# Four early pairs of feature tiles in a decoder-layer kernel, their low parts left by accumulating DMAs

## The chip, the cores and the metric

The kernel runs on one core of a Trainium2 chip. The metric is the device time of one execution in microseconds (us), as the median of several runs. In the profile, PE is the matrix engine (TensorE), PEld its weight loads, DVE the vector engine, ACT the scalar engine, POOL the GpSimd engine and SP the engine that issues the kernel's DMAs.

## What is computed

One decoder layer on x of 512 tokens by 1024 features, in float32. Cut to what matters here:

```python
def reference(x, ...):
    mix = hybrid_mixer(x, w_in, ...)                # attention (8 heads) and a gated MLP (8 groups), then w_out
    x = layer_norm(ALPHA * x + mix, ln1_g, ln1_b)   # the first layer norm
    ffn = (silu(x @ w_gate) * (x @ w_up)) @ w_down  # hidden width 2816: 22 feature tiles of 128
    return layer_norm(ALPHA * x + ffn, ln2_g, ln2_b)
```

## The kernel before, in words

**Precision.** Each float32 operand is split in two float32r parts, high = round(a) and low = a - high, and a product is three matmuls: high by high, high by low, low by high. `split` (lines 234 to 241) issues the two operations: an ACT copy for the high part (line 238), and a subtraction on DVE or POOL for the low part (line 239; POOL with `far=True`). `mm3` (lines 243 to 249) is the three matmuls of the projections (lines 245 to 247).

**Stages.** In order of time: the projections v, q, k, z, u mixed with attention and the gated MLP; the output projection in two halves, `out_half(4, ...)` for the gated MLP and `out_half(0, ...)` for attention; the first layer norm, token tile by token tile (`layer_norm`, lines 679 to 713, called from `pa_done`, line 746), with transposes of the normalised rows (line 760) and splits of them; gate and up projections; down projection; the second layer norm.

**The attention half.** `pa_done` adds the projection, scaled by the token's RMS factor `ra[t]`, to xk (line 750). `ra[t]` comes from four calls of `rsqrt_col` (line 672): a small DVE operation (line 274) and a power operation on POOL (line 275) for each token tile. The letter of `LN1 = "APAD"` for token tile t says who normalises it: A and P use ACT (line 700) and then DVE for the gain (line 702), with the bias added on DVE (A) or POOL (P) at line 711; D uses DVE alone (lines 696 and 707).

**Gate and up projection.** The 22 feature tiles go in 11 pairs. A pair's weights are four blocks of 128x1024 (`Raw`, 512 KB each: a11, a21, a22, a12), and a pair takes seven products of 24 matmuls each (`product`, matmuls at line 838) in the manner of Strassen and Winograd: P1, P2, p5, p6, p3, p7, q4. Each has an operand made from the normalised tokens: P1 (`b11`) and P2 (`b21`) need only token tiles 0 and 1; `b22`, `n1`, `n2`, `t3` and `t4` need tiles 2 and 3 and the sums of `combine` (lines 728 to 741). The product P1 goes to a PSUM bank X, is copied by ACT to a tile `a` with the tag "cs" (line 860), and P2 is added on top in X; ACT's silu (line 865) and a DVE product (line 866) follow. P1 and P2 use the raw blocks a11 and a12; the other five use block sums (`grow`, line 933) or raw blocks. A split block takes one of three buffers "wh" and one of three "wl".

**Early pairs.** The first two pairs have P1 and P2 made ahead of the loop over pairs (lines 908 to 913), so that PE has them to do while the layer norm of token tiles 2 and 3 and `combine` go on. Their split blocks have buffers of their own, left by attention and the gated MLP ("pth" and "ptl" for the high parts, "znh" and "znl" for the low ones), and all four low parts are made on POOL (`EPOOL`). The raws of pair 0 and 1 come in through two "wr" buffers and two slots of "zg"; pair 0's a11 and a12 stay in their buffers for the loop. The loop then makes P1 and P2 for pairs 2 to 10 only.

**Order.** No instruction order is written by hand. Each operation is entered with an engine, a cost in us and a rank, and `Order.plan` (lines 107 to 177) simulates the five queues as a list scheduler: an engine that is free takes the ready operation with the lowest rank. The order in which the operations are issued, and with it each engine's in-order queue, is fixed by these planned costs. `MM = 0.643` is the planned cost of one `mm3`, a DMA has 1.9 us of latency after its issue, and tiles of one tag wait in the order of their creation for a buffer to come free.

Of the kernel before, what the change touches and what calls it, by code (L numbers as in the profile page):

```python
# [6 lines left out]
F32 = mybir.dt.float32  # L7
F32R = mybir.dt.float32r
AF = mybir.ActivationFunctionType
# [20 lines left out]

SAME, CROSS, DMA_LAT, MM, MM256 = 0.15, 0.19, 1.9, 0.643, 0.36
SEQ = ('q1', 'a1', 'q0', 'z', 'q2', 'a0', 'u', 'q3', 's', 'a2', 'a3')
RANK = {"w": 5.0, "rope": 10.0, "att": 4.0, "gelu": -8.0, "z": -2.0, "s": -13.5, "fill": 15.0, "sq": -6.0, "ln": -10.5, "ffn": 8.0, "evac": 3.0}


UNITS = (2, 0, 3, 1)
NORM = "AADA"
LN1, LN2, LNT = "APAD", "ADAD", 0.3  # L40
WHI = ('o0', 'o2', 'q1')
WPOOL = ('e0', 'e1', 'e3', 'o1', 'o2', 'o4', 'z')
ROPE, ZSUB, ZMUL, ZG, ZB = "P", "P", "P", "P", "P"
# [18 lines left out]
class Order:  # L62
# [11 lines left out]
        b.name = f"{b.tag}_{self.uid}"  # L74
        return b

    def op(self, eng, cost, fn, r=(), w=(), base=None, table=None, lock=False):
        o = Op()
        o.eng, o.cost, o.fn, o.table, o.lock = eng, cost, fn, table, lock
        o.lat = DMA_LAT if eng == "SP" else 0.0  # L80
        o.prio = (self.base if base is None else base, len(self.ops))
        o.deps, o.succ, o.bufs = set(), [], []
        for keys, writes in ((r, False), (w, True)):
            for key in keys:
                b, sub = key if isinstance(key, tuple) else (key, None)
                if not b.users:
                    self.bufs.append(b)
                if not b.users or b.users[-1] is not o:
                    b.users.append(o)
                    o.bufs.append(b)  # L90
                for s, x in b.writers.items():
                    if x is not o and (s is None or sub is None or s == sub):
                        o.deps.add(x)
                if writes:
                    for s, xs in b.readers.items():
                        if s is None or sub is None or s == sub:
                            o.deps.update(x for x in xs if x is not o)
                    if sub is None:
                        b.writers, b.readers = {None: o}, {}
                    else:  # L100
                        b.writers[sub], b.readers[sub] = o, []
                else:
                    b.readers.setdefault(sub, []).append(o)
        self.ops.append(o)
        return o
# [80 lines left out]
def build(tc, cp, wp, ap, ps, xt, xtok, w_vqk, w_zu, w_out, w_gu, w_dn, wsp, cst, rows, cols, out):  # L186
# [8 lines left out]
    def dve(n, fn, r, w, per=1.042, **k):  # L195
        od.op("DVE", 0.066 + 0.001 * per * n, fn, r, w, **k)
# [10 lines left out]
    def const(shape, tag=None, dtype=F32):  # L207
        return od.buf(cp, shape, dtype, tag)
# [10 lines left out]
    def small(n):  # L219
        return work([P, n], "sm", 24)  # L220

    def bank(tag, bufs):
        return od.buf(ps, [P, S], F32, tag, bufs)
# [10 lines left out]
    def split(n, src, hi, lo, rs, ws_hi, ws_lo, far=False, lock=True, near=False, **k):  # L234
        if near:
            dve(n, lambda: V.tensor_scalar(hi(), src(), 1.0, None, op0=ALU.mult), rs, ws_hi, per=0.52, lock=True, **k)
        else:
# [2 lines left out]
                                                                 op=ALU.subtract), [*rs, *ws_hi], ws_lo,  # L240
               lock=lock, **k)

    def mm3(cost, o, lh, ll, rh, rl, start, stop, r, w, **k):
        def fn():
            PE.matmul(o(), lhsT=lh(), rhs=rh(), start=start, stop=False)  # L245
            PE.matmul(o(), lhsT=lh(), rhs=rl(), start=False, stop=False)  # L246
            PE.matmul(o(), lhsT=ll(), rhs=rh(), start=False, stop=stop)  # L247

        pe(cost, fn, r, w, **k)
# [27 lines left out]


    ident, tri = const([P, P]), const([P, 2 * P])
    cosT, sinT = od.buf(cp, [P, S], F32, "cs", 2), od.buf(cp, [P, S], F32, "cs", 2)  # L280
    colp, rowp = const([P, 12]), const([P, 3, S])
    mhalf, ones = const([P, 32]), const([P, 2])
    dve(32, lambda: V.memset(mhalf.t, -0.5), [], [mhalf])
# [6 lines left out]
        return b  # L290


    zero, idle = const([P, S], dtype=mybir.dt.bfloat16), bank("pv", 1)
    dve(256, lambda: V.memset(zero.t, 0.0), [], [zero], base=-9)

    def warm():
# [350 lines left out]
    out_half(4, "zg", sg_left, pg_done)  # L647


    sb, ra = bank("tp", 1), [small(1) for _ in range(NT)]  # L650
    at2 = work([P, 2, NT, S], "xh", 1, F32R)

    def at_split(f):
# [14 lines left out]

    pe(0.45, sums, [sqa, ones], [sb], base=RANK["s"])
    od.base = RANK["att"]  # L670
    for t in range(NT):
        rsqrt_col(ra[t], lambda t=t: sb.t[:, t:t + 1], [sb], 1, 1.0 / 512, RMS_EPS)
    od.base = RANK["fill"]

    LN = [row(0), row(1)]
# [70 lines left out]
    def pa_done(t, b):  # L746
        ts = slice(t * P, t * P + P)

        def add(i, key):
            dve(560, lambda: V.scalar_tensor_tensor(out=xk.t[:, t, HV[i]], in0=b[i].t, scalar=ra[t].t,  # L750
                                                    in1=xk.t[:, t, HV[i]], op0=ALU.mult, op1=ALU.add),
                [b[i], ra[t], key], [key])

        def done(i, key):
            tp = bank("tp", 1) if i == 0 else bank("pv", 1)

            def turn():
                for j in range(4):
                    js = slice((4 * i + j) * P, (4 * i + j + 1) * P)
                    PE.transpose(tp.t[:, j * P:j * P + P], xk.t[:, t, js], ident.t)  # L760

            pe(0.45, turn, [*key, ident], [tp])
            xr = XR[i, t] = prob() if t < 2 else tmp()
            act(512, lambda: A.activation(xr.t, tp.t, AF.Copy), [tp], [xr])
            if t < 2 or i == 1:
                opnd_split(("b11", "b21")[i] if t < 2 else "b22", t % 2,
                           lambda: tp.t.rearrange("p (k c) -> p k c", c=P), [tp], False)
            if t >= 2 and i == 1:
                combine(t - 2)

        od.base = RANK["ln"] + LNT * t
        layer_norm(t, add, done, LN1[t])
        od.base = RANK["fill"]
# [22 lines left out]
    class Raw:  # L796


        def __init__(self, p, j, slot):
            if slot in ("wr", "kl"):  # L800
                b = od.buf(wp, [P, WCH], F32, "wr", 2) if slot == "wr" else work([P, WCH], "kl", 2)
                self.t, self.key = (lambda c=slice(0, WCH): b.t[:, c]), b
            else:
                self.t, self.key = (lambda c=slice(0, WCH): zgr.t[:, slot, c]), (zgr, slot)
            dma(512, lambda: nc.sync.dma_start(self.t(), w_gu[4 * p + j]), [], [self.key], base=PREP)

    class Blk:


        def __init__(self, early=None):  # L810
            if early is None:
                h, l = od.buf(wp, [P, WCH], F32R, "wh", 3), od.buf(wp, [P, WCH], F32R, "wl", 3)
                self.lo, self.lk = (lambda c: l.t[:, c]), l
            else:
                h, l = work([P, WCH], ("pth", "ptl")[early // 2], 2, F32R), early_lo[early // 2]
                self.lo, self.lk = (lambda c: l.t[:, early % 2, c]), (l, early % 2)
            self.hi, self.hk = (lambda c: h.t[:, c]), h
# [6 lines left out]
            return self  # L824

    def whole(raw, early=None):
        return Blk(early).fill(raw.t, raw.key, far=early in EPOOL)

    def product(blk, name, bank, first):
        buf, s = OPND[name]  # L830
# [15 lines left out]
    class Pair:  # L846
# [4 lines left out]
            (self.h0, self.i0), (self.h1, self.i1) = hT[2 * p], hT[2 * p + 1]  # L851

        def begin(self):
            self.a = od.buf(cp, [P, S], F32, "cs", 2)
            self.X = pj()

        def p1(self, blk):
# [47 lines left out]
            self.gated(c, self.h1, self.i1, 0, -1.0)  # L905

    pairs = [Pair(p) for p in range(NP)]
    EARLY, EPOOL = 2, (0, 1, 2, 3)
    first = [[Raw(0, 0, "wr"), Raw(0, 3, "wr")], [Raw(1, 0, 0), Raw(1, 3, 1)]]
    for p in range(EARLY):  # L910
        blks = [whole(r, 2 * p + i) for i, r in enumerate(first[p])]
        pairs[p].p1(blks[0])
        pairs[p].p2(blks[1])
    RING = ("kl", "kl", "wr", "wr", 0, 1)
    held_back = None
    for p, pair in enumerate(pairs):
        if p == 0:
            a11, a12 = first[0]
            a21, a22 = Raw(0, 1, 0), Raw(0, 2, 1)
        else:  # L920
            a11, a21, a22, a12 = (Raw(p, j, RING[(4 * (p - 1) + j) % 6]) for j in range(4))
        if p >= EARLY:
            pair.p1(whole(a11))

        acc = [bank("tp", 1), bank("pv", 1)]
        s1 = Blk()

        def grow(blk, one, two):
            for side in range(2):
                def step(side=side, o=acc[side]):  # L930
                    x = (lambda: o.t) if two is None else (lambda: two.t(HALF[side]))
                    k = [o] if two is None else [two.key]
                    dve(512, lambda: V.tensor_tensor(out=o.t, in0=x(), in1=one.t(HALF[side]), op=ALU.add),
                        [one.key, *k], [o], lock=two is not None, base=PREP)
                    blk.fill(lambda: o.t, o, 512, 512 * side, lock=False)

                step()

        grow(s1, a21, a22)
        pool(1024, lambda a=a11, b=a21: PL.tensor_tensor(out=b.t(), in0=a.t(), in1=b.t(), op=ALU.add),  # L940
             [a11.key, a21.key], [a21.key], base=PREP)
        pair.p5(s1)
        if held_back:
            held_back[0].q4(held_back[1])
        s2 = Blk()
        grow(s2, a11, None)
        pair.p6(s2)
        if p >= EARLY:
            pair.p2(whole(a12))
        s4 = Blk()  # L950
        grow(s4, a12, None)
        pair.p3(s4)
        pair.p7(whole(a21))
        held_back = pair, whole(a22)
# [123 lines left out]
```

## Time and profile before

| | |
|---|---|
| median of 3 runs | 570.67 us (569.95 to 571.86) |
| the profiled execution's own time | 570.17 us |
| its span in the trace | 568.1 us |
| PE busy | 547.5 us, 96% of the span |
| DVE busy | 413.2 us, 73% |
| ACT busy | 280.9 us, 49% |
| POOL busy | 157.0 us, 28% |

The profile is of one execution. The span runs from its first to its last recorded instruction; times inside it are counted from the span's start. Busy shares are averages over stages with different limits, so the stage around the first layer norm is read from windows and timelines of its own.

### The profile page before, as it was taken

Reading aid. Unit: us, or ns where it says so; the run is one execution under the profiler, and the core shown is the slowest. Engines: PE = TensorE matmul, PEld = TensorE weight load, DVE = VectorE, ACT = ScalarE, POOL = GpSimd, SP = SyncE. Lnnn points to the kernel's source line nnn. Section 1 sums busy time; section 2 is a strip of 40 time slices with the busy share of each in tenths; the row PEclk is TensorE's granted clock in tenths of the full one; section 3 lists DMA queues with packets and bytes.
Section 4 is the critical chain, followed back from the end, with each engine's and each line's share of the span. In section 5 each row is a group of like instructions: output and inputs, shape, how many; then the busy total and the mean of one; then the engine's idle time right before and its main releaser. Section 6 shows DMA issues by size and latency. Waiting matters only on the chain.

```text
span 568.1 us, 8774 instructions
## 1 busy us (share of the span) xinstructions
PE 547.5 (96%) x3360; PEld 488.6 (86%) x3360; DVE 413.2 (73%) x707; ACT 280.9 (49%) x482; POOL 157.0 (28%) x119
## 2 busy tenths in 40 slices
PE   9999999999899968999999999999999999999994
PEld 5888888887688857999999999999999888888883
DVE  5537779879975699998788788888877723334385
ACT  6323796788864347544545544544455422323211
POOL 0026258613205730253333242343322200000011
PEclk9999999999999979899999999999999999999998
DMA  7745514155715201432332333333124332232311
GB/s 260 265 131 153 140 48 129 43 163 182 226 38 194 102 3 72 144 127 103 112 112 76 115 109 109 116 111 112 38 75 149 112 111 94 92 112 74 112 74 74
DMA packets 21225, 65.51 MB, mean 115 GB/s; under 512 B 2880, under 2 KB 3392, under 8 KB 21184
## 3 DMA queue, kind: packets, MB, share of 16 engines
q1 hardware_dynamic: 21184, 64.96, 34.6%
q8 instruction: 26, 0.43, 0.3%
q14 instruction: 15, 0.12, 0.1%
HBM read 58.66 MB, written 2.10 MB: 107 GB/s over the span
## 4 chain that ended last, share of the span: by engine, by line
PE 94%; DVE 2%; ACT 2%; issue 0%; POOL 0%; DVEq 0%
PE pj L838 22%; PE sc L838 17%; PE pj L245 12%; PE pj L247 12%; PE pj L246 12%; PE sc L245 2%; PE sc L247 2%; PE sc L246 2%; PE pv L481 2%; PE tp L464 1%; PE sc L426 1%; PE pv L247 1%; PE pv L245 1%; PE tp L247 1%; PE tp L245 1%; PE tp L246 1%
## 5 line engine op out<-in xcount | busy, mean ns | idle before, releaser
L239 DVE TENSOR_TENSOR wl<-wr,wh 128x1024 fp32r<-128x1024 f32 (+1 forms) x55 | 71.8, 1306 | 60.7 <-ACT wh L238 60.1
L238 ACT ACTIVATE wh<-wr 128x1024 fp32r<-128x1024 f32 (+1 forms) x58 | 57.8, 999 | 84.4 <-PE sc L247 54.0
L838 PE MATMUL pj<-qk,wh 128*128 128x256 f32 x352 | 65.6, 287 | 1.2 <-ACT wh L238 1.2
L838 PE MATMUL sc<-xh,wh 128*128 128x256 f32 x352 | 64.5, 284 | 0.0
L838 PEld LDWEIGHTS pj<-qk,wh 128*128 128x128 f32 x352 | 55.8, 195 | 1.4 <-ACT wh L238 1.4
L838 PEld LDWEIGHTS sc<-xh,wh 128*128 128x128 f32 x352 | 55.1, 193 | 0.0
L275 POOL TENSOR_TENSOR sm<-sm,only 128x1 f32<-128x1 f32 (+1 forms) x20 | 16.4, 825 | 137.8 <-DVE sm L274 137.7
L838 PE MATMUL pj<-V,wh 128*128 128x256 f32 x288 | 52.6, 283 | 0.0
L838 PE MATMUL pj<-qk,wl 128*128 128x256 f32 x176 | 50.7, 288 | 0.4 <-DVE wl L239 0.4
L838 PE MATMUL sc<-xh,wl 128*128 128x256 f32 x176 | 49.8, 283 | 0.0
L245 PE MATMUL pj<-wh,xh 128*128 128x512 f32 x114 | 46.3, 406 | 0.0
L838 PEld LDWEIGHTS pj<-V,wh 128*128 128x128 f32 x288 | 44.9, 192 | 0.0
L246 PE MATMUL pj<-wl,xh 128*128 128x512 f32 x114 | 44.6, 391 | 0.0
L838 PE MATMUL pj<-V,wl 128*128 128x256 f32 x144 | 40.8, 283 | 0.0
L247 PE MATMUL pj<-wh,xl 128*128 128x512 f32 x96 | 37.7, 393 | 0.0
L239 POOL TENSOR_TENSOR wl<-wr,wh 128x1024 fp32r<-128x1024 f32 x7 | 17.2, 2456 | 72.8 <-ACT wh L238 67.9
L838 PEld LDWEIGHTS pj<-qk,wl 128*128 128x128 f32 x176 | 34.3, 195 | 0.8 <-DVE wl L239 0.8
L838 PEld LDWEIGHTS sc<-xh,wl 128*128 128x128 f32 x176 | 33.9, 192 | 0.0
L238 ACT ACTIVATE wh<-tp 128x512 fp32r<-128x512 f32 x33 | 19.7, 596 | 27.9 <-PE sc L838 26.0
L838 PE MATMUL sc<-ug,wh 128*128 128x256 f32 x176 | 32.1, 283 | 0.0
L239 DVE TENSOR_TENSOR wl<-tp,wh 128x512 fp32r<-128x512 f32 x33 | 22.6, 684 | 8.6 <-ACT wh L238 8.6
L245 PE MATMUL pj<-wh,pr 128*128 128x512 f32 x72 | 28.0, 389 | 0.0
(331 smaller groups left out, 1512.1 us busy)
## 6 DMA issues: line engine op xcount, KB each, us to landing
wr<-w_dn SPq DMA_DIRECT2D x22, 512.0 KB, 3.2
zg<-w_gu SPq DMA_DIRECT2D x16, 512.0 KB, 3.4
wr<-w_gu SPq DMA_DIRECT2D x16, 512.0 KB, 3.5
kl<-w_gu SPq DMA_DIRECT2D x14, 512.0 KB, 3.3
wr<-w_vqk SPq DMA_DIRECT2D x8, 512.0 KB, 3.6
wr<-w_zu SPq DMA_DIRECT2D x8, 512.0 KB, 3.3
wr<-w_out SPq DMA_DIRECT2D x8, 512.0 KB, 4.1
wr<-w_vqk SPq DMA_DIRECT2D x8, 256.0 KB, 4.0
```

The lines of the kernel that those rows point to most:

```text
L238: act(n, lambda: A.activation(hi(), src(), AF.Copy), rs, ws_hi, **k)
L239: either("P" if far else "D", n, lambda E: E.tensor_tensor(out=lo(), in0=src(), in1=hi().bitcast(F32), op=ALU.subtract), [*rs, *ws_hi], ws_lo,
L245: PE.matmul(o(), lhsT=lh(), rhs=rh(), start=start, stop=False)
L246: PE.matmul(o(), lhsT=lh(), rhs=rl(), start=False, stop=False)
L247: PE.matmul(o(), lhsT=ll(), rhs=rh(), start=False, stop=stop)
L275: od.op("POOL", 0.3 + 0.165 * n, lambda: PL.tensor_tensor(out=o.t, in0=v.t, in1=mhalf.t[:, :n], op=ALU.pow), [v, mhalf], [o], lock=True)
L426: PE.matmul(sc.t[:, :n], lhsT=qs.t[:, e, ts], rhs=ks.t[:, 2 * e + 1, :n], start=False, stop=True)
L464: PE.transpose(tp.t[:, j * P:j * P + P], p.t[:, j * P:j * P + P], ident.t)
L481: PE.matmul(pv.t[:, j * P:], lhsT=vs.t[:, j, h, :], rhs=pt.t[:, j * S:j * S + w], start=j == 0 and i == 0, stop=j == NT - 1 and i == 1)
L838: PE.matmul(o, lhsT=lh(w), rhs=buf.t[:, s + rh, x], start=first and side == k == i == 0, stop=k == 3 and i == 2, skip_group_check=True)
```

## The change

- `EARLY` goes from 2 to 4: pairs 0 to 3 have P1 and P2 made ahead of the loop. Blocks 4 to 7 (pairs 2 and 3) use the common buffers "wh" and "wl". The raws come through "wr", "zg", "wr", "zg", and the loop loads all four raws of pair 0 anew. The tag "cs" has 4 buffers in place of 2.
- The low parts of all eight early blocks (`EARLY_LO = "MMMMMMMM"`) are made by `split_dram`: ACT copies the raw block to the high part, copies it again with scale -1 into the low part's tile, and a DMA issued on POOL's queue adds the raw block from DRAM to it. The planner is told 0.9 us for the issue and 10 us of latency.
- The four `rsqrt_col` calls for `ra` become one, over four columns.
- Token tile 3 of the first layer norm is normalised in manner A, not D.
- `MM` goes from 0.643 to 0.681 for the planner. The tile of zeros for the first matmuls moves to the tag "kl".

```diff
-SAME, CROSS, DMA_LAT, MM, MM256 = 0.15, 0.19, 1.9, 0.643, 0.36
+SAME, CROSS, DMA_LAT, MM, MM256 = 0.15, 0.19, 1.9, 0.681, 0.36
+GROW, GROW_LAT = 0.9, 10
...
-LN1, LN2, LNT = "APAD", "ADAD", 0.3
+LN1, LN2, LNT = "APAA", "ADAD", 0.3
...
+    def split_dram(n, src, dram, hi, lo, rs, ws_hi, ws_lo, **k):
+
+        act(n, lambda: A.activation(hi(), src(), AF.Copy), rs, ws_hi, **k)
+        act(n, lambda: A.activation(lo(), src(), AF.Copy, scale=-1.0), rs, ws_lo, **k)
+        od.op("POOL", GROW, lambda: nc.gpsimd.dma_start(lo(), dram, accum_op=ALU.add), ws_lo, ws_lo, lat=GROW_LAT, **k)
...
-    cosT, sinT = od.buf(cp, [P, S], F32, "cs", 2), od.buf(cp, [P, S], F32, "cs", 2)
+    cosT, sinT = od.buf(cp, [P, S], F32, "cs", 4), od.buf(cp, [P, S], F32, "cs", 4)
...
-    zero, idle = const([P, S], dtype=mybir.dt.bfloat16), bank("pv", 1)
+    zero, idle = work([P, S], "kl", 2, mybir.dt.bfloat16), bank("pv", 1)
...
-    for t in range(NT):
-        rsqrt_col(ra[t], lambda t=t: sb.t[:, t:t + 1], [sb], 1, 1.0 / 512, RMS_EPS)
+    rsqrt_col(ra, lambda: sb.t[:, 0:NT], [sb], NT, 1.0 / 512, RMS_EPS)
...
-            if early is None:
+            if early is None or early > 3:
                 h, l = od.buf(wp, [P, WCH], F32R, "wh", 3), od.buf(wp, [P, WCH], F32R, "wl", 3)
...
     def whole(raw, early=None):
-        return Blk(early).fill(raw.t, raw.key, far=early in EPOOL)
+        how = "D" if early is None else EARLY_LO[early]
+        if how != "M":
+            return Blk(early).fill(raw.t, raw.key, far=how == "P")
+        b, c = Blk(early), slice(0, WCH)
+        split_dram(WCH, raw.t, raw.src, lambda: b.hi(c), lambda: b.lo(c), [raw.key], [b.hk], [b.lk], base=PREP)
+        return b
...
-    EARLY, EPOOL = 2, (0, 1, 2, 3)
-    first = [[Raw(0, 0, "wr"), Raw(0, 3, "wr")], [Raw(1, 0, 0), Raw(1, 3, 1)]]
+    EARLY, EARLY_LO = 4, "MMMMMMMM"
+    EARLY_SLOTS = (("wr", "wr"), (0, 1), ("wr", "wr"), (0, 1))
     for p in range(EARLY):
-        blks = [whole(r, 2 * p + i) for i, r in enumerate(first[p])]
+        blks = [whole(Raw(p, 3 * i, EARLY_SLOTS[p][i]), 2 * p + i) for i in range(2)]
         pairs[p].p1(blks[0])
         pairs[p].p2(blks[1])
...
         if p == 0:
-            a11, a12 = first[0]
-            a21, a22 = Raw(0, 1, 0), Raw(0, 2, 1)
+            a21, a22 = Raw(0, 1, "wr"), Raw(0, 2, "wr")
+            a11, a12 = Raw(0, 0, 0), Raw(0, 3, 1)
```

## Rows read from the trace of the kernel before

**Rows 1.** The page: busy time of each engine; share of the chain by engine.

```profile
PE 547.5 (96%) x3360; PEld 488.6 (86%) x3360; DVE 413.2 (73%) x707; ACT 280.9 (49%) x482; POOL 157.0 (28%) x119
...
PE 94%; DVE 2%; ACT 2%; issue 0%; POOL 0%; DVEq 0%
```

**Rows 2.** Windows: start:end, length, busy us by engine, PE clock, DMA share, GB/s.

```profile
138.00:142.00 4.00, 2.99 (x17) 2.08 (x16) 4.00 (x10) 3.95 (x11) 0.45 (x1) 1.00 0.67 202
142.00:146.00 4.00, 2.43 (x10) 1.42 (x10) 3.53 (x7) 4.00 (x9) 2.10 (x2) 1.00 0.88 315
...
200.50:208.50 8.00, 2.93 (x16) 2.00 (x14) 7.47 (x16) 4.54 (x8) 4.51 (x5) 0.85 0.01 2
208.50:213.00 4.50, 4.35 (x19) 4.00 (x19) 4.46 (x9) 2.49 (x5) 0.13 (x1) 0.51 0.07 7
213.00:221.00 8.00, 8.00 (x71) 8.00 (x70) 6.93 (x13) 6.26 (x11) 0.00 (x0) 1.00 0.34 128
221.00:227.80 6.80, 3.51 (x29) 3.10 (x27) 6.58 (x13) 5.11 (x10) 0.00 (x0) 1.00 0.00 0
227.80:233.00 5.20, 4.80 (x25) 4.37 (x26) 5.07 (x9) 2.35 (x4) 2.38 (x1) 0.71 0.04 9
233.00:262.00 29.00, 29.00 (x242) 29.00 (x242) 26.09 (x37) 14.73 (x25) 12.51 (x9) 0.99 0.48 160
```

**Rows 3.** Timeline of PE around the layer norm: start, length, instruction, [idle before <-releaser].

```profile
189.84 0.39 PE L247 MATMUL pj<-ug,xh 128*128 128x512 f32 x1
...
206.27 1.11 PE L760 MATMUL tp<-only,xl 128*128 128x128 f32 x4 [4.96 <-POOL xl L711]
...
208.56 1.31 PE L838 MATMUL pj<-V,pth 128*128 128x256 f32 x2
...
223.41 0.51 PE L838 MATMUL pj<-V,ptl 128*128 128x256 f32 x2 [2.05 <-ACT cs L860]
...
227.80 0.50 PE L838 MATMUL pj<-qk,wh 128*128 128x256 f32 x2 [1.25 <-ACT wh L238]
...
232.96 0.59 PE L838 MATMUL sc<-xh,wh 128*128 128x256 f32 x2
```

**Rows 4.** The chain in order of time: one product of the loop (start, length).

```profile
250.58 2.88 PE pj L838 x24
```

**Rows 5.** Timeline of DVE in the same stage.

```profile
191.19 1.41 DVE L750 SCALAR_TENSOR_TENSOR xl<-pj,sm,xl 128x512 f32<-128x512 f32 x2 [3.46 <-POOL sm L275]
...
197.06 0.20 DVE L688 BATCH_NORM_AGGREGATE sm<-sm 128x2 f32<-128x12 f32 x1
...
200.20 0.15 DVE L274 TENSOR_SCALAR sm<-sm 128x1 f32<-128x1 f32 x1
```

**Rows 6.** Timeline of POOL in the same stage.

```profile
188.25 2.40 POOL L239 TENSOR_TENSOR znh<-wr,pth 128x1024 fp32r<-128x1024 f32 x1
190.61 2.11 POOL L275 TENSOR_TENSOR sm<-sm,only 128x1 f32<-128x1 f32 x4
...
204.47 2.97 POOL L711 TENSOR_TENSOR xl<-xl,kl 128x512 f32<-128x512 f32 x2 [3.49 <-DVE xl L702]
```

**Rows 7.** Timeline of ACT in the same stage.

```profile
188.64 1.06 ACT L238 ACTIVATE pth<-wr 128x1024 fp32r<-128x1024 f32 x1 [2.08 <-DMA wr<-w_gu]
...
202.83 1.53 ACT L700 ACTIVATE xl<-xl,sm,sm 128x512 f32<-128x512 f32 x2
207.42 0.60 ACT L764 ACTIVATE pr<-tp 128x512 f32<-128x512 f32 x1 [3.05 <-PE tp L760]
...
213.92 0.60 ACT L860 ACTIVATE cs<-pj 128x512 f32<-128x512 f32 x1 [2.79 <-PE pj L838]
```

**Rows 8.** DMA issues: destination and source, count, KB each, median us to landing.

```profile
wr<-w_gu SPq DMA_DIRECT2D x16, 512.0 KB, 3.5
...
qk<-qk SPq DMA_DIRECT2D x8, 256.0 KB, 3.3
```

**Rows 9.** Timeline of the SP queue: the last early raw.

```profile
188.32 0.33 SPq L805 DMA_DIRECT2D zg<-w_gu  x1
```

More of the change, by code (lines that the diff above doesn't have):

```diff
@@ L75, in buf, with op @@
         return b
-    def op(self, eng, cost, fn, r=(), w=(), base=None, table=None, lock=False):
+    def op(self, eng, cost, fn, r=(), w=(), base=None, table=None, lock=False, lat=0.0):
         o = Op()
         o.eng, o.cost, o.fn, o.table, o.lock = eng, cost, fn, table, lock
-        o.lat = DMA_LAT if eng == "SP" else 0.0
+        o.lat = DMA_LAT if eng == "SP" else lat
         o.prio = (self.base if base is None else base, len(self.ops))
@@ L647, in build @@
     out_half(4, "zg", sg_left, pg_done)
-    sb, ra = bank("tp", 1), [small(1) for _ in range(NT)]
+    sb, ra = bank("tp", 1), small(NT)
     at2 = work([P, 2, NT, S], "xh", 1, F32R)
@@ L749, in add @@
         def add(i, key):
-            dve(560, lambda: V.scalar_tensor_tensor(out=xk.t[:, t, HV[i]], in0=b[i].t, scalar=ra[t].t,
+            dve(560, lambda: V.scalar_tensor_tensor(out=xk.t[:, t, HV[i]], in0=b[i].t, scalar=ra.t[:, t:t + 1],
                                                     in1=xk.t[:, t, HV[i]], op0=ALU.mult, op1=ALU.add),
-                [b[i], ra[t], key], [key])
+                [b[i], ra, key], [key])
         def done(i, key):
@@ L804, in __init__ @@
                 self.t, self.key = (lambda c=slice(0, WCH): zgr.t[:, slot, c]), (zgr, slot)
-            dma(512, lambda: nc.sync.dma_start(self.t(), w_gu[4 * p + j]), [], [self.key], base=PREP)
+            self.src = w_gu[4 * p + j]
+            dma(512, lambda: nc.sync.dma_start(self.t(), self.src), [], [self.key], base=PREP)
     class Blk:
         def __init__(self, early=None):
-            if early is None:
+            if early is None or early > 3:
                 h, l = od.buf(wp, [P, WCH], F32R, "wh", 3), od.buf(wp, [P, WCH], F32R, "wl", 3)
@@ L853, in begin @@
         def begin(self):
-            self.a = od.buf(cp, [P, S], F32, "cs", 2)
+            self.a = od.buf(cp, [P, S], F32, "cs", 4)
             self.X = pj()
```

## The prediction

> **What bounds the kernel now.** I read the page first. PE is busy for 96% of the span and makes up 94% of the chain of work that ended last [rows 1]. Little can come from making any other engine faster as such; time can come only from stretches in which PE stands still or runs at its lower clock. The table of windows shows where these lie [rows 2]. The loop over pairs has none: from 233 to 262 us PE is busy for 29.00 of 29.00 us at a granted clock of 0.99. The first layer norm has three. From 200.5 to 208.5 PE works 2.93 of 8.00 us. From 208.5 to 213 it works, at a clock of 0.51, so at the lower of its two levels (1.2 GHz), after that standstill. From 221 to 227.8 it works 3.51 of 6.80 us, and the next 5.2 us run at a mean clock of 0.71.
>
> PE's timeline says what each waits for [rows 3]. The transposes of token tile 1 wait 4.96 us for its bias on POOL. At 223.41 PE has waited 2.05 us for ACT's copy of X, and at 227.80 another 1.25 us for the first block of the loop: P1 and P2 of two pairs are used up before `combine` and the block sums are ready. DVE is the reason: it is busy 6.58 of those 6.80 us [rows 2].
>
> **The change, part by part.** The sum is made against the profiled execution, 570.17 us, 0.5 below the median of 570.67; the 0.5 is added at the end.
>
> *Two more pairs early.* A product takes 2.88 us at full clock [rows 4]. P1 and P2 of pairs 2 and 3 are four products, 11.5 us, moved from the loop to the stage where PE runs dry; the work of PE as a whole is the same. What is gained is what they fill. Idle: 2.05 + 1.25 = 3.30 us [rows 3]. Clock: the first product of the loop runs from 227.80 to 232.96 [rows 3], 5.16 us where 2.88 would do, so 2.28 us (a wait of 0.40 us inside it counted). Together 5.6 us. 11.5 us of cover is ample for 3.3 us of gaps, so PE should run through from 208.5 into the loop. What is late next stays: the 4.96 us at 206.27, and the low clock until 213, since no product can start before token tiles 0 and 1 are normalised.
>
> *The loop gets denser.* Pairs 2 and 3 then have five products, 14.4 us each, in place of 20.2. Two such pairs stand in the trace already: pairs 0 and 1 are the ten products from 233 to 262 us, with DVE at 26.09 of 29 us, POOL at 12.51 and the DMA share at 0.48 [rows 2]. I cost it at 0. If DVE needed 10% more there, it would be the bound, and each dense pair would cost about 1.4 us.
>
> *ACT copies.* Each early block takes two copies of 1.06 us [rows 7] where it took one: 16 copies in place of 4, so 12 more or 12.7 us. They lie in ACT's idle time: between 188.64 and 228 us ACT has gaps such as 3.05 us before 207.42 and 2.79 us before 213.92 [rows 7]. But between 200.9 and 204.4 ACT is itself on the way to token tile 1's transposes (its normalisation is at 202.83 [rows 7]), and a copy started just before holds that up by up to 1.06 us. I take one such hit: +1.0 us, ends 0 and +3.2 (three blocks).
>
> *Low parts.* Four subtractions of 2.40 us leave POOL [rows 6]; eight DMA issues come to it. No issue on POOL's queue is in the trace. Bounds: 0.33 us as on SP [rows 9], and 2.40 us, the operation that it replaces; I take 1.0, nearer to the issue. The landing of an accumulating transfer is not there either. The lower end is a plain load of the same 512 KB, 3.5 us [rows 8]. The upper end adds a read of 512 KB from SBUF: 256 KB from SBUF to SBUF take 3.3 us [rows 8], so 6.6 us, and 10.1 in all. I take 7. When is each needed? Blocks 0 to 3 have their raws by about 192 us (the last issue is at 188.32 [rows 9]) and are needed from 208.56 [rows 3]. Blocks 4 to 6 need buffers that the output projection leaves near 200 us, are copied in ACT's gaps up to 214, and are needed from about 224: 208.56, four products, 11.5, and 4.3 for clock and transposes. Block 7 waits for a buffer until P1 of pair 2 is done, about 227; copies 2.1, issue 1.0, landing 7: 237. By then PE has P2 of pair 2, P1 of pair 3, and p5 and p6 of pair 0, up to 238.8. Covered, by 1.7 us; with a landing of 10.1 us the 1.4 us that are short have p7 as cover. SP loads six more raws of 512 KB; its queue and the DMA engines are idle here (share 0.00 to 0.34 [rows 2]).
>
> A row first: from 200.5 to 227.8 us DVE is hardly ever idle, and the POOL operation at 204.47 takes 2.97 us for two tiles of 512, in that company [rows 2, 6]. The rule: the Trainium skill (SBUF — State Buffer, Who interferes with whom, and the table of rules at its end) says that a DMA issued by GpSimd needs GpSimd to write its descriptors, that DVE in a two-port mode locks it out, and that such a DMA should not be hidden under DVE work. By it the landings would be several times 3.5 us and the sum would turn positive. The same page says that `tensor_tensor` has no two-port mode, and no run here shows either case.
>
> *The power operation.* The first layer-norm addition waits 3.46 us for `ra`, up to 191.19 [rows 5]. Its power operations start at 190.61, behind a subtraction of 2.40 us [rows 6], and in the new kernel POOL has no such subtraction. The matmuls that it also needs end about 190.2 [rows 3]. So DVE's chain starts up to 0.9 us earlier: I take -0.7, ends 0 and -0.9.
>
> *Token tile 3 in manner A.* Two ACT operations (1.53 us [rows 7]) more; on DVE four operations of about 0.7 us stay four. Tile 3 is no longer what PE waits for; 0, ends -0.5 and +0.5.
>
> *MM and the zeros.* The planner's order may move anywhere. The stretch that shows what this can be worth is 138 to 146 us, where PE works 5.42 of 8.00 us [rows 2]: ends -2.6 and +2.6, and I take 0. The tile of zeros is free long before its buffer is wanted: 0.
>
> **Sum:** -5.6 + 1.0 - 0.7 = -5.3, and 0.2 for small waits of the longer buffer queue: -5.1. 570.17 - 5.1 = 565.1; with 0.5, **565.6 us**. A measurement of this kernel can tell 0.3%, 1.7 us, from no change.
>
> **The rivals.**
>
> *Late low parts (slower).* The accumulating transfers run one behind another on POOL's queue, each for X us. The first can start near 182 us; block 6, the seventh, lands at 182 + 7X and is wanted at 230 (224.3 and two products). The gain is eaten where 182 + 7X = 230 + 5.1, so at X = 7.6. At X = 8.5 PE waits until 241.5: 11.5 late, 6.4 slower, 577 us. For it: X may lie anywhere between 3.5 and 10.1, and DVE is busy throughout. Against: the DMA engines are nearly idle (share 0.00 to 0.34 in the stage) and plain loads overlap. The Trainium skill's rule above is one way to such an X.
>
> *The gain is given back in the layer norm (no change).* From 200.5 to 227.8 us ACT is busy for 18.4 of 27.3 us (four windows of [rows 2]); six more copies, two more normalisations, two more copies of X bring it to about 27 (6.4 + 1.5 + 1.2 more). With three copies in front of tile 1 (+3.2), and a POOL queue in which an issue that waits for ACT stands ahead of the bias at 204.47 (+1.0), P1 starts 4.2 us later: -5.6 + 4.2 = -1.4, 569.3 us. For it: each queue is in order, and ACT has the longest list of new work. Against: the copies have a lower rank than the layer norm.
>
> *The first gap shrinks too (faster still).* Tile 1's variance is known at 197.06 but used at 200.20, behind tile 0's gain and bias on DVE [rows 5]. A new order that puts it first would save about 2.6 us of the 4.96 and some of the low clock after it, 1 us: 562.0 us. For it: the planner's costs change. Against: the ranks do not.
>
> **How the numbers follow.** The forecast has 0.53, late low parts 0.14, given back 0.20, the first gap 0.13. The forecast's own range is 565.6 with -3 (no ACT hit, a better order before 186 us) and +3: 562.6 to 568.6. The range goes to 560.5, which leaves out about 0.06 of the best case, and to 572.0, which takes in the second rival with the planner's +2.6, and leaves out most of the late low parts. Faster by over 0.3%: 0.53 and 0.13, and 0.04 of the second rival: 0.70. Within: 0.13 of the second rival. Slower: 0.14 and 0.03: 0.17.
>
> **What would show it.** Right: no idle PE and a clock of 1.00 from 213 us to the end of the loop; P1 of pair 2 right behind P2 of pair 1; the loop's pairs 2 and 3 at 14.4 us; accumulating DMAs landing within 10 us. Wrong: PE waiting for a DMA into "znh", "znl" or "wl"; tile 1's transposes later than 206.3; DVE late for pair 2 or 3; new waits ahead of 186 us.

## The result, and the profile after

The changed kernel takes 566.93 us (median of 14 runs) against 571.33 for the kernel before on the same chips: a ratio of 0.9927 [0.9901, 0.9952], 4.2 us less by the ratio and 4.4 between the medians. The profiled execution took 566.79 us with a span of 565.0, 3.1 less than before's 568.1. So the time came out 1.3 us above the forecast. The way there was another one in several places.

The page of the changed kernel, as [rows 1], and its DMA issues on POOL's queue, as [rows 8] (the last number is the median time to landing in us):

```profile
PE 545.7 (97%) x3360; PEld 488.1 (86%) x3360; DVE 406.6 (72%) x701; ACT 290.0 (51%) x492; POOL 158.2 (28%) x120
...
wl<-w_gu POOLq DMA_DIRECT2D x4, 512.0 KB, 7.1
znl<-w_gu POOLq DMA_DIRECT2D x2, 512.0 KB, 9.3
znh<-w_gu POOLq DMA_DIRECT2D x2, 512.0 KB, 12.8
```

The windows of the changed kernel, with the columns of [rows 2]:

```profile
138.00:142.00 4.00, 3.27 (x20) 2.69 (x18) 4.00 (x10) 3.84 (x10) 1.28 (x1) 1.00 0.91 231
142.00:146.00 4.00, 0.33 (x1) 0.14 (x1) 3.54 (x7) 3.08 (x7) 1.00 (x1) 0.69 0.84 284
146.00:150.00 4.00, 3.00 (x11) 2.36 (x11) 2.78 (x6) 3.94 (x9) 2.37 (x2) 0.50 0.99 375
150.00:154.00 4.00, 4.00 (x15) 2.97 (x13) 3.84 (x10) 1.67 (x4) 1.38 (x2) 0.53 1.01 363
...
201.00:209.00 8.00, 7.59 (x42) 6.17 (x40) 5.99 (x12) 5.99 (x10) 3.10 (x3) 1.00 1.05 274
209.00:215.00 6.00, 4.48 (x33) 4.08 (x33) 4.72 (x9) 5.25 (x8) 0.88 (x1) 1.00 0.93 229
215.00:221.00 6.00, 5.91 (x49) 5.73 (x50) 5.11 (x11) 5.98 (x11) 2.30 (x3) 1.00 0.88 186
221.00:228.00 7.00, 6.39 (x55) 6.19 (x54) 6.36 (x12) 4.93 (x9) 0.00 (x0) 1.00 0.96 263
228.00:236.00 8.00, 7.88 (x66) 7.68 (x65) 8.00 (x15) 6.63 (x13) 3.52 (x2) 1.00 0.41 110
```

The reader is to see three things. First, from 201 to 236 us PE is busy for 32.25 of 35 us and its clock is 1.00 throughout, where before it stood still for 5 us at tile 1 and 3.3 us before the loop and ran at 0.51 and 0.71 behind that [rows 2]. Second, a new loss stands near the end of attention: from 142 to 146 us PE works 0.33 of 4 us, and until 154 it runs at about half clock; before, PE lost 2.6 us from 138 to 146 us and its clock stayed at 1.00 [rows 2]. Third, the DMA engines, idle in this stage before, are full: their share is 0.88 to 1.05 from 201 to 228 us.

PE's timeline shows what it waits for in the new loss, two operations on DVE:

```profile
143.29 0.33 PE L471 MATMUL tp<-only,pr 128*128 128x128 f32 x1 [2.02 <-DVE sm L281]
...
146.35 1.12 PE L591 MATMUL pj<-only,ug 128*128 128x128 f32 x4 [2.74 <-DVE ug L586]
```

PE's timeline around the layer norm, as [rows 3]:

```profile
205.47 0.60 PE L766 MATMUL tp<-only,xl 128*128 128x128 f32 x4
205.82 0.48 PE L252 MATMUL pj<-wh,xh 128*128 128x512 f32 x1
...
209.51 0.39 PE L850 MATMUL pj<-V,pth 128*128 128x256 f32 x1 [0.92 <-ACT V L239]
...
220.86 0.40 PE L850 MATMUL pj<-V,wh 128*128 128x256 f32 x2
...
224.14 0.51 PE L850 MATMUL pj<-V,ptl 128*128 128x256 f32 x2 [0.61 <-ACT cs L872]
...
234.10 0.40 PE L850 MATMUL pj<-qk,wh 128*128 128x256 f32 x2
...
249.96 0.47 PE L850 MATMUL sc<-ug,wh 128*128 128x256 f32 x2 [0.92 <-ACT wh L239]
```

Products of the output projection (line 252) now stand between the transposes of tile 0 and those of tile 1, and between the two halves of tile 1's (line 766), so the wait of 4.96 us is gone. The third early pair's first product starts at 220.86 with its block from "wh", and p5 of the loop follows at 234.10 without a wait.

To compare orders that differ everywhere, I cut each profiled span at two marks: DVE's first addition of the layer norm, and the first matmul of P1. The first two columns of times are starts in the profiled execution, the third is the span less P1's start.

| kernel | first addition | P1 starts | P1 to the end | median | ratio to before |
|---|---|---|---|---|---|
| before | 191.2 | 208.6 | 359.5 | 570.8 to 571.7 | 1 |
| changed | 192.6 | 209.5 | 355.5 | 566.93 | 0.9927 [0.9901, 0.9952] |
| e1 changed, MM 0.643 | 190.6 | 213.2 | 356.1 | 569.93 | 0.9980 [0.9962, 0.9997] |
| e2 before, MM 0.681 | 194.1 | 212.4 | 366.7 | 580.95 | 1.0161 [1.0134, 1.0188] |
| e3 changed, two early pairs | 192.5 | 208.2 | 366.4 | 576.70 | 1.0104 [1.0083, 1.0125] |
| e4 changed, lows on POOL | 192.0 | 216.2 | 357.5 | 576.78 | 1.0108 [1.0080, 1.0136] |
| e5 e1, raws planned later | 192.7 | 212.6 | 356.0 | 567.34 | 0.9930 [0.9903, 0.9956] |
| e6 changed, MM split | 187.5 | 203.2 | 358.9 | 564.17 | 0.9889 [0.9859, 0.9920] |
| e7 changed, four powers | 193.0 | 208.9 | 355.1 | 567.06 | 0.9924 [0.9898, 0.9950] |
| e8 changed, APAD | 193.5 | 210.2 | 355.4 | 567.06 | 0.9917 [0.9894, 0.9939] |
| e9 e6, two early pairs | 189.6 | 205.3 | 364.7 | 570.17 | 0.9972 [0.9952, 0.9992] |
| e10 before, MM split | 192.0 | 208.3 | 362.4 | 573.39 | 1.0031 [1.0009, 1.0053] |
| e11 e6, lows on DVE | 188.6 | 207.2 | 356.9 | 565.67 | 0.9897 [0.9871, 0.9923] |
| e12 e6, three early pairs | 189.3 | 205.0 | 361.7 | 568.62 | 0.9948 [0.9923, 0.9973] |

The kernel before was timed beside each batch (570.83, 571.52 and 571.65 for e1 to e4, e5 to e8 and e9 to e12). The ratios are taken over all executions, so they need not be the quotient of two medians (e6 is the case in point: two of its six executions lie 2.4 and 4.3 us above its median). One of e10's twelve executions, 906.28 us at a mean clock of 0.56, is left out of its row. The profiled executions lie within 1.6 us of their medians, except e5's, which is 3.0 us above. Each edit is planned anew, so each run holds the edit and a new order.

### The profile page after: what moved, and what is told of

Its sections match the earlier page's. It is cut to its first block, busy times and chain, and to the rows that moved or that the text cites. A ratio compares the mean times of both kernels' runs of the same rounds, so it can differ in the third digit from the quotient of the medians.

```text
span 565.0 us, 8788 instructions
## 1 busy us (share of the span) xinstructions
PE 545.7 (97%) x3360; PEld 488.1 (86%) x3360; DVE 406.6 (72%) x701; ACT 290.0 (51%) x492; POOL 158.2 (28%) x120
## 4 chain that ended last, share of the span: by engine, by line
PE 84%; DMA 5%; ACT 5%; DVE 3%; issue 2%; SPq 1%; POOL 0%; DVEq 0%; POOLq 0%; ACTq 0%
PE pj L850 19%; PE sc L850 16%; PE pj L252 11%; PE pj L253 11%; PE pj L254 11%; DMA wr<-w_gu 2%; PE sc L252 2%; PE sc L253 2%; PE sc L254 2%; PE pv L488 2%; PE tp L471 1%; DMA wr<-w_out 1%; DMA zg<-w_gu 1%; DMA qk<-qk 1%; PE pv L252 1%
## 5 line engine op out<-in xcount | busy, mean ns | idle before, releaser
L850 PE MATMUL pj<-qk,wh 128*128 128x256 f32 x352 | 64.4, 283 | 0.0
L282 POOL TENSOR_TENSOR sm<-sm,only 128x1 f32<-128x1 f32 (+2 forms) x17 | 18.7, 1099 | 124.8 <-DVE sm L281 124.8
L850 PEld LDWEIGHTS sc<-ug,wh 128*128 128x128 f32 x176 | 27.5, 192 | 1.2 <-ACT wh L239 1.1
L253 PE MATMUL pj<-wl,pr 128*128 128x512 f32 x72 | 28.0, 390 | 0.0
```

The costliest lines, as they stand in the source:

```text
L282: od.op("POOL", 0.3 + 0.165 * n, lambda: PL.tensor_tensor(out=o.t, in0=v.t, in1=mhalf.t[:, :n], op=ALU.pow), [v, mhalf], [o], lock=True)
L850: PE.matmul(o, lhsT=lh(w), rhs=buf.t[:, s + rh, x], start=first and side == k == i == 0, stop=k == 3 and i == 2, skip_group_check=True)
```

## The experiments

**e1 and e2: the planner's MM alone.**

```diff
# e1, in the changed kernel
-SAME, CROSS, DMA_LAT, MM, MM256 = 0.15, 0.19, 1.9, 0.681, 0.36
+SAME, CROSS, DMA_LAT, MM, MM256 = 0.15, 0.19, 1.9, 0.643, 0.36
# e2, in the kernel before: the other way round
```

> The changed kernel with the planner's MM back at 0.643. Theory A (the early pairs make the gain; MM only moves PE's standstill from the layer norm to the end of attention, for about nothing): PE stands still at the layer norm again (about 5 us near 201 to 207) with the low clock behind it, and hardly at 142 to 146 us; P1 starts within 1 us of 208.6; from P1 to the end about 355 to 357 us; time 565.5 to 568. Rival B (the new MM makes the gain, by the output projection's products that now cover the layer norm): 569.5 to 571.5.

> The kernel before with MM at 0.681 and nothing else. Theory A: the standstill moves to 142 to 146 us, the stretch from 201 to 209 us is filled by the output projection, the gaps before the loop (3.3 us) stay; time within 2 us of before, 569.5 to 573. Rival B: 566 to 568.

Theory A failed in both. e1 came out in the range of rival B, and e2 far above either range. With the rest of the change, the new MM is worth 3.0 us (569.93 to 566.93); without it, it costs 10 us (570.83 to 580.95). The other parts give 0.9 us at 0.643 and 14 at 0.681. No part's price stands by itself.

In e1 the early pairs do their work (356.1 us from P1 to the end, 3.4 less than before), but P1 starts 4.7 us later than before. ACT's timeline of e1 shows why:

```profile
204.29 1.06 ACT L246 ACTIVATE wh<-wr 128x1024 fp32r<-128x1024 f32 x1 [2.98 <-DMA wr<-w_gu]
205.25 0.58 ACT L770 ACTIVATE pr<-tp 128x512 f32<-128x512 f32 x1
...
207.16 1.53 ACT L706 ACTIVATE xl<-xl,sm,sm 128x512 f32<-128x512 f32 x2
```

A copy of an early block waits 2.98 us for its raw load, and tile 0's copies (line 770) and tile 1's normalisation (line 706) stand behind it in ACT's queue. The load itself was slow: issued at 195.96, it landed after 8.3 us, where a plain load of that size takes 3.4 (median), beside an accumulating transfer issued at 196.22 that took 8.9. PE then waits 6.37 us for tile 1. A part of rival B's mechanism is in it too: the products of the output projection end at 204.3, and PE has none left to cover that wait.

In e2, windows of the same form show what 0.681 does to the kernel before: the loss near 142 us with a low clock, and a second one before the loop.

```profile
138.00:154.00 16.00, 11.02 (x47) 8.51 (x46) 14.79 (x32) 13.47 (x30) 5.47 (x5) 0.79 0.94 307
200.00:215.00 15.00, 11.35 (x54) 8.93 (x53) 14.37 (x24) 6.07 (x10) 8.07 (x6) 0.91 0.11 35
215.00:240.00 25.00, 18.35 (x118) 17.71 (x118) 21.48 (x38) 14.41 (x26) 2.90 (x2) 0.77 0.13 44
```

**e3: two early pairs in the changed kernel.**

```diff
-    EARLY, EARLY_LO = 4, "MMMMMMMM"
+    EARLY, EARLY_LO = 2, "MMMMMMMM"
```

> The changed kernel with two early pairs instead of four, their low parts still by accumulating DMAs. Theory A: at least 2.5 us of idle PE between the second pair's P2 and the loop, and a fall of the clock behind it; 4 to 6 us above the changed kernel: 570 to 573. Rival B: within 1.5 us of the changed kernel, 566 to 568.5.

9.8 us above the changed kernel, past the upper end of what theory A expected (6); rival B is out. Up to P1 the run is like the changed one (208.2 to 209.5). The time is lost after it, and PE's timeline of e3 shows where:

```profile
221.44 0.80 PE L850 MATMUL pj<-V,ptl 128*128 128x256 f32 x2 [3.25 <-ACT cs L872]
...
227.95 0.84 PE L850 MATMUL pj<-qk,wh 128*128 128x256 f32 x2 [1.02 <-ACT wh L239]
...
232.35 0.58 PE L850 MATMUL pj<-qk,wl 128*128 128x256 f32 x1 [3.56 <-DVE wl L240]
```

These three waits are 7.8 us in all.

**e4: low parts on POOL.**

```diff
-    EARLY, EARLY_LO = 4, "MMMMMMMM"
+    EARLY, EARLY_LO = 4, "PPPPPPPP"
```

> The changed kernel with the low parts of the eight early blocks subtracted on POOL (2.4 us each, 19 us in all) instead of left by DMAs. Theory A (the DMAs matter by freeing POOL's queue): the bias of token tile 1 and the power operations wait behind subtractions, P1 starts 1 to 3 us later, blocks 4 to 6 come late; 1 to 4 us above the changed kernel: 568 to 571. Rival (the way the low parts are made is hidden either way): within 1 us of the changed kernel.

The mechanism of theory A, at more than twice the upper end of its size (4): 9.9 us. POOL's timeline of e4 has the subtractions ahead of tile 1's bias (line 717), and DVE's has its own addition slowed beside them:

```profile
203.37 5.61 POOL L240 TENSOR_TENSOR wl<-wr,wh 128x1024 fp32r<-128x1024 f32 x2
208.93 2.35 POOL L240 TENSOR_TENSOR wl<-zg,wh 128x1024 fp32r<-128x1024 f32 x1
212.17 2.88 POOL L717 TENSOR_TENSOR xl<-xl,kl 128x512 f32<-128x512 f32 x2 [0.90 <-DVE xl L708]
```

```profile
201.07 5.69 DVE L717 TENSOR_TENSOR xl<-xl,kl 128x512 f32<-128x512 f32 x2
```

Those two DVE additions take 1.29 us in the changed kernel. P1 starts at 216.2, 6.7 us late.

**e5: the planner told nearer the truth about the raw loads.** Only planned latencies differ from e1: 7.9 us in place of 1.9 for the raws of early pairs 2 and 3, where the late one in e1 took 8.3.

```diff
-        blks = [whole(Raw(p, 3 * i, EARLY_SLOTS[p][i]), 2 * p + i) for i in range(2)]
+        blks = [whole(Raw(p, 3 * i, EARLY_SLOTS[p][i], 6.0 if p > 1 else 0.0), 2 * p + i) for i in range(2)]
```

> The changed kernel with MM at 0.643, and the planner told 6 us more latency for the raw loads of early pairs 2 and 3 (the loads themselves are the same). Theory C (with MM at 0.643 the gain was given back because an early-block copy that waits for its raw load stands ahead of token tile 0's copies and tile 1's normalisation in ACT's queue): those ACT operations now come first, tile 1's transposes start 3 us or more earlier than 210.7, P1 by 210.5; 2 to 4 us below that run: 566 to 568. Rival D (the layer norm is late for another reason, and the wait goes to POOL's bias or DVE): 569 to 571.

The time fell by 2.6 us to 567.34, as theory C had it. The profile, of the slowest of e5's six executions (570.33), agrees in part: P1 comes 19.8 us after the first addition in place of 22.6, but at 212.6 it is later than theory C's 210.5 and near e1's, since in this execution the layer norm itself began 2.1 us later; and PE still waits 3.5 us for tile 1's bias on POOL, which rival D had. So the copy in ACT's queue was a part of the delay, and not all of it.

**e6: MM split.** `MM = 0.643` for the projections, `MMO = 0.681` in the `mm3` calls of the output and down projections.

```diff
-                        mm3(MM, lambda: b[hf].t, lh, ll, ...
+                        mm3(MMO, lambda: b[hf].t, lh, ll, ...
...
-        mm3(MM, lambda: yb[t][hf].t, ...
+        mm3(MMO, lambda: yb[t][hf].t, ...
```

> The changed kernel with MM at 0.643 for the projections up to the end of attention, and 0.681 only for the output and down projections. Theory E (0.681 costs time near 142 to 154 us, through attention's order, and its good side is the order of the output projection and of ACT's copies behind it): standstill near 142 to 150 us at most 3 us and no low clock there; early-block copies behind tile 1's normalisation; P1 at 207 to 209; 355 to 357 us from P1 to the end; 563 to 566. Rival F (what is gained near 146 us is lost again as standstill before tile 1's transposes, since the layer norm's own chain sets P1's start): P1 at 209 or later, 566 to 569.

564.17 us, within theory E's range, with the lowest ratio of all. It is faster than e1. Against the changed kernel the intervals overlap, so that it is faster than that one is likely, but not shown. The windows of e6:

```profile
138.00:154.00 16.00, 13.06 (x69) 9.56 (x68) 15.39 (x30) 13.66 (x29) 3.41 (x5) 1.00 0.73 230
200.00:215.00 15.00, 13.51 (x104) 12.77 (x103) 12.67 (x26) 12.99 (x20) 4.58 (x6) 1.00 0.93 223
215.00:240.00 25.00, 24.00 (x197) 23.39 (x196) 21.77 (x35) 16.61 (x28) 3.28 (x2) 1.00 0.68 187
```

No low clock is left near 150 us; the first addition comes 5.1 us earlier than in the changed kernel, and P1 at 203.2, nearly 4 us earlier than the 207 to 209 that E had. Rival F falls: the time saved near 146 us was not lost again before tile 1. It gave back 3.4 us after P1 (358.9 for 355.5; E had 355 to 357). PE's waits there are 1.49 and 0.33 us for ACT's copies of X, 0.62 for DVE and three of 0.87 in the dense pairs of the loop, 5.1 us in all for 2.6 in the changed kernel. The first of the three:

```profile
243.99 0.47 PE L850 MATMUL sc<-ug,wh 128*128 128x256 f32 x2 [0.87 <-DVE rt L856]
```

**e7 and e8: the two small parts, each undone in the changed kernel** (four calls of `rsqrt_col`; `LN1 = "APAD"`).

> The changed kernel with the four separate power operations for ra, as before. Theory: in the changed kernel the first addition waits for PE and not for ra, so the three further power operations (about 1.7 us of POOL) are mostly hidden: within 1.5 us of the changed kernel, 565.5 to 568.5. Rival (the single operation made part of the gain): 569 or more, the first addition waiting for POOL.

> The changed kernel with token tile 3 normalised on DVE alone again. Theory: tile 3 is hidden behind P1 and P2 of four pairs: within 1.5 us of the changed kernel, 565.5 to 568.5, with PE's waits before the loop no longer than 2 us in all. Rival (ACT is short of time in this stage, so less work for it helps): 563 to 565; or DVE is (it helps the other way): 569 or more.

Both 567.06 us, 0.1 from the changed kernel: neither part moves the time here by more than the intervals allow, about 1.4 us. In e7 the four power operations end at about the time when PE delivers; the addition waits for PE all the same (DVE's timeline of e7):

```profile
192.96 1.41 DVE L757 SCALAR_TENSOR_TENSOR xl<-pj,sm,xl 128x512 f32<-128x512 f32 x2 [2.09 <-PE pj L254]
```

**e9, e10 and e12: the early pairs again, in e6's setting.** e9 has `EARLY = 2`, e12 `EARLY = 3`, both in e6; e10 is the kernel before with the two MM values of e6.

> The kernel of e6_mm_split with two early pairs instead of four. Theory A (two more early pairs fill what PE lacks before the loop): idle PE of 3 us or more between the second pair's P2 and the loop, the clock falling behind it; 3 to 8 us above e6: 567 to 572. Rival B (once the order is good, the early pairs add nothing): within 1.5 us of e6, 563 to 565.7.

> The kernel before with the split MM (0.643, and 0.681 for the output and down projections) and nothing else. Theory A: the order of the layer norm may be better, but the gaps before the loop stay: 566 to 572, with 360 us or more from P1 to the end. Rival B (the order alone makes e6's time): 563 to 565.7.

> The kernel of e6_mm_split with three early pairs. By the gaps (3.3 us idle and 2.3 us of low clock before, against 5.8 us of work in one more pair) three should nearly do: within 2 us of e6, 562.5 to 566, with fewer waits of PE for DVE in the loop's first pairs. Rival (the fourth pair is needed too): 566.5 or more, idle PE before the loop.

e9 is 6.0 us above e6 (4.7 by the ratios), with P1 to the end at 364.7 for 358.9; e10, at 573.39, is 1.8 us slower than before by its ratio. So the split order alone gives nothing and four early pairs are what makes it pay. Theory A holds in e9, though PE's idle time came as four waits of 2.18, 0.82, 1.29 and 0.36 us at and in the loop's first product and not as one. In e10 rival B is out and theory A's gaps are there (362.4 from P1 to the end), but the time lies above A's range. e12 missed its range and came out in the rival's: with three pairs the time is 568.62, 4.4 above e6 (3.4 by the ratios), with PE idle for 1.75 us before the loop and for 3.27 us in it. My reckoning from the gaps before (5.6 us, one pair's work) was too small: ACT's copy of the loop's first block releases PE at 230.6 in e12 and at 227.8 before, although P1 started 3.6 us earlier. Why that copy comes so late was not followed further.

**e11: the low parts on DVE.**

```diff
-    EARLY, EARLY_LO = 4, "MMMMMMMM"
+    EARLY, EARLY_LO = 4, "DDDDDDDD"
```

> The kernel of e6_mm_split with the eight low parts subtracted on DVE (1.2 us each, 9.8 us in all) instead of left by accumulating DMAs. Theory G (DVE has no time to spare in this stage, so the DMAs are what makes room for four early pairs): token tiles 2 and 3 and the block sums come later, 3 to 9 us above e6: 567 to 573. Rival H (PE has so much early work that DVE's delay is hidden): within 1.5 us of e6.

1.5 us above e6, at the edge of rival H: theory G falls. P1 starts 4.0 us later (207.2), behind a wait of 2.65 us for tile 1's bias, but P1 to the end is 2.0 us shorter, and the ratios differ by 0.0008 with wide overlap. The accumulating DMAs are not what makes room for four early pairs; e4 and e11, though in different settings, say that keeping the subtractions off POOL is enough.

## Why the prediction was right or wrong

**The early pairs** (-5.6). Right in kind. Undone alone they cost 9.8 us (e3) and 6.0 us (e9), where MM was 0.681 or split; with MM at 0.643 all parts together gave only 0.9 us (e1). The changed kernel's P1 to the end is 4.0 us shorter than before's. What the 5.6 left out on either side: the clock no longer falls before P1 (the 0.51 from 208.5 to 213 [rows 2] is 1.00 now), which gives about 2.1 us by that row (an estimate); and new waits of 0.3 to 0.9 us at ACT, DVE and the loop, 2.6 us in all from 209.5 (0.34 + 0.74 + 0.61 + 0.92), which take it back. That sum is 5.1, and the other 1.1 us up to the 4.0 measured stay open.

**"What is late next stays: the 4.96 us at 206.27, and the low clock."** Wrong. The wait is gone, since products of the output projection now stand between the transposes. This is the third rival's gap, closed in another way than it said: not by DVE's order, but by PE's.

**MM, taken as 0 with ends of 2.6.** This is the step that failed most. The bound came from PE's idle time between 138 and 146 us and did not hold the clock that falls after a longer standstill, nor the layer norm's order. Measured: -3.0 us with the rest of the change and +10 without it. From 138 to 154 us PE works 10.5 to 11.2 of 16 us in all six kernels with 0.681 everywhere (changed, e2, e3, e4, e7, e8), and 13.0 to 13.3 in all eight where the projections have 0.643. The two long waits of this stretch, 2.02 and 2.74 us in the changed kernel, stand in e2 as 2.19 and 2.56, so it is the new MM that brings them. That the sum came near is partly chance: two changes that the sum does not have nearly cancel. One is the new loss, in the windows of before and of the changed kernel:

```profile
138.00:154.00 16.00, 13.29 (x71) 9.93 (x71) 15.37 (x32) 13.72 (x29) 3.65 (x5) 1.00 0.77 242
138.00:154.00 16.00, 10.60 (x45) 8.16 (x43) 14.16 (x30) 12.52 (x27) 6.03 (x5) 0.68 0.94 313
```

PE is idle for 2.7 us more, and from 146 to 154 us it does 7.00 us of work at a mean clock of 0.51: about 6 us lost. The other is the gap at tile 1 that closed: 4.96 us of idle time and the same 2.1 us of low clock behind it as above, about 7 us. Both are estimates from these rows.

**The dense loop, taken as 0.** Nearly: one wait of 0.92 us in the changed kernel, three of 0.87 in e6, less than the 1.4 per pair of the bound. The bound was worked wrongly: 10% more DVE work would be 28.7 of the 29.00 us, still under PE.

**ACT's copies** (+1.0, end 3.2). Right in size, at another place. P1 comes 16.9 us after the first addition in the changed kernel, 0.5 less than before, since the gap at tile 1 closed, but a hit is there. ACT's timeline of the changed kernel:

```profile
206.48 1.06 ACT L246 ACTIVATE wh<-wr 128x1024 fp32r<-128x1024 f32 x1 [1.91 <-DMA wr<-w_gu]
207.45 1.04 ACT L247 ACTIVATE wl<-wr 128x1024 fp32r<-128x1024 f32 x1
208.40 0.57 ACT L770 ACTIVATE pr<-tp 128x512 f32<-128x512 f32 x1
208.87 0.59 ACT L239 ACTIVATE V<-tp 128x512 fp32r<-128x512 f32 x1
```

Tile 1's first transposes start at 205.47, and ACT's copies of them stand behind two copies of an early block, the first of which waited for its raw load. PE waits 0.92 us for them at 209.51, right ahead of P1. In e1 the hit was larger: one such copy waited 2.98 us for its raw load ahead of the layer norm. That is the second rival's mechanism, with its outcome: e1's 569.93 for the rival's 569.3. I priced a copy by its duration, and not by the load that it waits for.

**Low parts.** The issue took 0.86 to 1.06 us for the 1.0 taken. Landing was 6.7 to 13.3 us for the 7 taken and an upper end of 10.1. "Its queue and the DMA engines are idle here" was wrong for the kernel after, and it is the step behind the hits on ACT: with 8 accumulating transfers and the raws of four pairs the share is 0.88 to 1.05, and the raw loads are in the same crowd. DMA issues of the changed kernel, first from 195 to 197 us, then from 232 to 234:

```profile
wr<-w_gu SPq DMA_DIRECT2D x1, 512.0 KB, 10.8
znh<-w_gu POOLq DMA_DIRECT2D x1, 512.0 KB, 12.3
...
zg<-w_gu SPq DMA_DIRECT2D x1, 512.0 KB, 3.6
wl<-w_gu POOLq DMA_DIRECT2D x1, 512.0 KB, 6.8
```

The load of 10.8 us, issued at 195.59, is the one for which ACT waits until 206.48. e11 has no accumulating transfers, and its DMA engines are far from full; the windows of e6 and then of e11:

```profile
200.00:208.00 8.00, 7.29 (x52) 6.55 (x50) 6.70 (x14) 6.02 (x9) 1.84 (x3) 1.00 1.04 270
200.00:208.00 8.00, 4.54 (x21) 3.05 (x19) 8.00 (x14) 5.79 (x10) 3.38 (x3) 0.93 0.22 68
```

From 176 to 212 us the raw loads landed in 3.2 to 5.8 us in e11 and in 3.3 to 12.2 in e6. So what the accumulating transfers cost, they cost by way of the raw loads. PE never waited for a low part itself in the changed kernel's profile, so late low parts did not come about. As to the rule of the Trainium skill (SBUF — State Buffer, Who interferes with whom), by which GpSimd cannot write descriptors under DVE's two-port work, no run here tests it. POOL's timeline of the changed kernel has an issue at 232.37, in the window in which DVE is busy 8.00 of 8.00 us, and it took no longer than the others; but DVE ran a `tensor_tensor` then (line 945, at 232.34), which the prediction had already set apart. The landings did come to 1.9 to 3.8 times the plain 3.5 us, but so did plain loads in the same crowd, and the sum did not turn positive:

```profile
232.37 0.86 POOL L248 DMA_DIRECT2D wl<-w_gu  x1 [13.97 <-ACT wl L247]
```

What did collide was POOL's arithmetic with DVE's, in e4 and once in the changed kernel (the last section).

**The power operation** (-0.7). Wrong in its mechanism: POOL has the power operation done at 191.87, but the first addition waits 1.62 us for PE, until 192.60, because PE came to that product of the output projection later. The time of e7, 0.1 off, could not have told 0.7 us by itself. **Token tile 3** (0): right within the noise (e8).

**The signs.** Of the signs of being wrong, new waits ahead of 186 us came, and the second half of tile 1's transposes at 207.99. Of the signs of being right, the landing within 10 us did not: three took 10.3 to 13.3.

## What to carry to other kernels

When a planner's costs set the order, a changed cost is a change of the whole program: measure it alone and with the other parts, and read where the standstill moved, since a longer one brings the low clock with it. Work moved ahead of a gap pays only while no in-order queue holds one of its operations, waiting for a load, in front of the work that makes the gap. Costs that differ by stage (here 0.643 and 0.681) can do better than one value everywhere, as e6 did against e1, but in the kernel before they cost time (e10). A transfer that takes work off an engine took DMA time from the loads beside it here: look at what waits for those.

## What was not expected of the hardware

An accumulating DMA of 512 KB from DRAM to SBUF landed in 6.7 to 13.3 us, against a median of 3.4 us for a plain load. Where the plain load issued beside it landed in 3.5 or 3.6 us, the accumulating one took 7.4 and 6.8 us, about twice (issued at 215.12 and 232.37). Where plain loads took 8.9 to 12.5 us, from 193.98 to 197.95, it took 10.3 to 13.3.

A POOL subtraction of 128x1024 held up DVE operations of 128x512. In e4 two additions took 5.69 us on DVE (for 1.29 together) beside two subtractions of 5.61 on POOL (for 2.40 each). The changed kernel has one such case, on DVE and on POOL:

```profile
186.80 2.86 DVE L665 SCALAR_TENSOR_TENSOR xh<-atr,only,xh 128x512 fp32r<-128x512 f32 x1
186.34 2.77 POOL L240 TENSOR_TENSOR wl<-wr,wh 128x1024 fp32r<-128x1024 f32 x1 [2.97 <-DVE wh L237]
```

The same DVE operation took 0.75 us before (line 658, at 185.30). DVE's subtraction at 233.87 kept to its usual 0.69 us beside a POOL operation of 2.77; it reads one of its two tiles from PSUM (`tp`), the held-up ones read both from SBUF. That a shared port is the reason was not tried here.
